# An attention layer's projections and value products with 512-column matmuls over both parts, the halves added afterwards, and its head transposes three steps behind

## The chip, the cores and the metric

The kernel runs on one core of a Trainium2 chip. The metric is the device time of one execution in microseconds, as the median of several runs. The core has five instruction streams: PE (TensorE, matmuls, with its weight loads shown apart as PEld), DVE (VectorE), ACT (ScalarE), POOL (GpSimd) and SP (which issues transfers). Each works through its own stream in order and waits for the others at semaphores.

## The reference

One inference step of a backbone of two layers over 9 tiles of 128 tokens: tile 0 is the context (128 tokens of a new request), tiles 1 to 8 are 1024 latent tokens. Layer 0 mixes tokens with retention and pooling, layer 1 with grouped-query attention; each is followed by a SwiGLU feed-forward part. The change lies in layer 1's attention:

```python
def attn_project(h, w_qkv, q_gain, k_gain):
    q, k, v = jnp.split(h @ w_qkv, [N_HEADS * HEAD_DIM, (N_HEADS + KV_HEADS) * HEAD_DIM], axis=-1)
    q = rmsnorm(q.reshape(B, T, N_HEADS, HEAD_DIM), q_gain)      # 8 heads of 128
    k = rmsnorm(k.reshape(B, T, KV_HEADS, HEAD_DIM), k_gain)     # 2 heads of 128
    v = v.reshape(B, T, KV_HEADS, HEAD_DIM)
    return q, k, v
...
qs, ksl = axial_rope(qs), axial_rope(ksl)                        # latent tokens only
k_all = jnp.concatenate([cache_k[:, j], ksl], axis=1)            # 256 cached + 1024 keys
v_all = jnp.concatenate([cache_v[:, j], vs], axis=1)
os_ = block_attention(qs, k_all, v_all) @ w_o[j]                 # softmax(q k^T * scale) v
```

The context tile attends to itself alone, and its normed keys and its values are outputs.

## The kernel before, in words

**Two parts.** The kernel works in float32, but its large matmuls use a faster format that keeps fewer bits. So every large operand is split into a high and a low part (`split`: ACT writes `hi`, a rounded copy; DVE writes `lo`, the source minus `hi`), and a product becomes three matmuls: high by high, high by low and low by high (`mm3`, whose matmul is line 182). A matmul takes a stationary operand of 128 x 128 and streams a moving operand of up to 512 columns past it. `mm3` accumulates all three products in the same columns of a PSUM bank. Layer 0 also uses another form, `mm_wide` (matmul on line 191): where the high and the low part of the moving operand lie at a fixed distance, one matmul with the high part as the stationary operand streams both, 256 + 256 columns, into the two halves of a bank; a second one, with the low part as the stationary operand, streams the high 256 columns into the first half. The halves are added when they are read (`add2`, lines 637 and 638: an ACT copy of one half to SBUF, then a DVE sum with the other half).

**Projections.** `blocks` lists six blocks of 256 output columns: `v`, q heads 0 and 1, `k`, and three more pairs of q heads. For each block and each of the 9 tiles, `qkv_step(bi, t)` multiplies the tile's hidden state (eight groups of 128 rows, in `h_hi`, `h_lo`) by the block's weights (`w_pair`) with `mm3`, 24 matmuls of 256 columns, into one of four banks in turn (in the last block banks 3 and 7). Blocks 0 and 1 are interleaved in groups of three tiles; the others follow one another. For `v` the result is then split into `VH`, `VL`. For `k` and `q`, ACT squares the result per head with an accumulator (line 1194), POOL makes the reciprocal root (`rstd_of`, lines 195 and 196), DVE scales the result into a buffer `qn` (line 1201), and the rotary part follows: a DVE product (1209), a POOL product (1210) and two DVE sums (1212, 1213). Then `qn` has to be transposed per head: `tail` does two PE transposes (line 1217) into bank 6 or 7 and a copy (line 1226) or split. The tail isn't issued at once but appended to `pend`, and a step issues the oldest tail behind its own matmuls when more than one is pending, so two steps later than its own. The buffers of `qn` rotate through three (`qnb`), those of the rotary parts through two (`rab`).

Between the projections stand side tasks: cached keys (`cached_k`) and values, and the context's own attention for each pair of heads (`ctx_pair`, at the places in `ctx_at`). In the last block, the first scores of the main loop are already issued (`q_split(0)`, `scores(0, ...)`).

**Attention.** The main loop runs over 32 `pairs` (8 tiles by 4 pairs of heads). For each: `q_split` on POOL; `scores`, per head, 9 or so matmuls over 1280 keys into two and a half banks, a DVE row maximum (1308), an ACT exponential (1310), a scaling on ACT (1315) or DVE (1313); `p_trans`, five calls of four transposes (1326) and a split, whose ACT copy is line 159 and whose DVE part is line 160; and `values`, five calls for 256 keys each, which accumulate over all five in bank 7, six matmuls of 256 columns in a call. After the last, an ACT copy (line 1344) takes bank 7 to `O`. The order within a pair is written out by hand, and runs into the pair before:

```python
for w in 'T0 v3 S0 T1 v4 T2 S1 T3 V0 V1 T4 V2'.split():
```

T is `p_trans`, S `scores` of the next pair, V `values` of this pair and v of the pair before.

**Order.** The order of the program is a priority. A scheduler at build time goes through it with modelled durations and gives each engine a fixed order, in which an instruction that is ready by the model can pass one that is not. It also sets the semaphores. Any two engines that use the same PSUM bank are kept apart.

Of the kernel before, what the change touches and what calls it, by code (L numbers as in the profile page):

```python
# [64 lines left out]
def hybrid_step_kernel(ctx: ExitStack, tc: tile.TileContext, a: dict, outs: list):  # L65
# [45 lines left out]
    def bank(i, n=1):  # L111
        return PS[:, i * 512:(i + n) * 512]
# [1037 lines left out]

    rope = XG[:, 0:2048].rearrange("p (t x) -> p t x", t=8)
    vctx = XG[:, 2048:2304]
    qnb = [XG[:, 2304 + 256 * i:2560 + 256 * i] for i in range(3)]
    rab = [XG[:, 3072 + 512 * i:3584 + 512 * i] for i in range(2)]
    kctx = T[:, 0:256]
    GQ = T[:, 512:768]
    jnk = [T[:, 256 + 128 * i:384 + 128 * i] for i in range(2)]
    VH = M2[:, 0:2048].rearrange("p (t e) -> p t e", t=8)
    VL = M2[:, 2048:4096].rearrange("p (t e) -> p t e", t=8)
    KR = M1.rearrange("p (v x s) -> p v x s", v=2, x=2)  # L1160
# [6 lines left out]
    pend = []  # L1167

    def qr_buf(bi, t, n):
        q, r = qnb[n % 3], rab[n % 2]  # L1170
        if bi == 5 and t > 3:
            q, r = RAW[:, 0, 256 * (n % 3):256 * (n % 3) + 256], RAW[:, 1, 512 * (n % 2):512 * (n % 2) + 512]
        return q, r[:, 0:256], r[:, 256:512]

    def qkv_step(bi, t):
        kind = blocks[bi][0]
        hi, lo = w_pair(2 * (bi % 2))
        g, j = divmod(t, 3)
        js = slice(j * 128, (j + 1) * 128)
        ps = bank(cnt["n"] % 4 if bi < 5 else 3 if t % 2 else 7)[:, 0:256]  # L1180
        cnt["n"] += 1
        mm3(ps, [(h_hi(g)[:, k, js], h_lo(g)[:, k, js], hi[:, k], lo[:, k]) for k in range(KD)])
        if len(pend) > 1:
            pend.pop(0)()
        if kind == "v":
            if t == 0:
                nc.scalar.copy(vctx, ps)
                nc.gpsimd.dma_start(out=new_cv[0, 0].rearrange("t v d -> t (v d)"), in_=vctx)
            else:
                split(VH[:, t - 1], VL[:, t - 1], ps)  # L1190
            return
        ss = sm(2)
        for e in range(2):
            nc.scalar.activation(jnk[e], ps[:, e * 128:(e + 1) * 128], ACTF.Square, accum_out=ss[:, e:e + 1])
        r = rstd_of(ss, 128, 2)
        cnt["q"] += 1
        n_qn = cnt["q"]
        qn, ra, rb = qr_buf(bi, t, n_qn)
        gain = GQ[:, 128:256] if kind == "k" else GQ[:, 0:128]
        for e in range(2):  # L1200
            nc.vector.scalar_tensor_tensor(qn[:, e * 128:(e + 1) * 128], ps[:, e * 128:(e + 1) * 128], r[:, e:e + 1],
                                           gain, op0=ALU.mult, op1=ALU.mult)
        if t == 0:
            if kind == "k":
                nc.gpsimd.dma_start(out=new_ck[0, 0].rearrange("t v d -> t (v d)"), in_=qn)
        else:
            v3 = lambda x: x.rearrange("p (h d) -> p h d", h=2)
            tb = rope[:, t - 1]
            nc.vector.tensor_mul(v3(ra), v3(qn), tb[:, 0:128].unsqueeze(1).to_broadcast([128, 2, 128]))
            nc.gpsimd.tensor_mul(v3(rb), v3(qn), tb[:, 128:256].unsqueeze(1).to_broadcast([128, 2, 128]))  # L1210
            v4 = lambda x: x.rearrange("p (q x i) -> p q x i", q=4, x=2)
            nc.vector.tensor_add(v4(qn)[:, :, 0], v4(ra)[:, :, 0], v4(rb)[:, :, 1])
            nc.vector.tensor_add(v4(qn)[:, :, 1], v4(ra)[:, :, 1], v4(rb)[:, :, 0])
        def tail(qn=qn, kind=kind, t=t, n=n_qn):
            tp = bank(6 + n % 2 if NT * bi + t < 4 * NT + 6 else 6)[:, 0:256]
            for e in range(2):
                nc.tensor.transpose(tp[:, e * 128:(e + 1) * 128], qn[:, e * 128:(e + 1) * 128], ident)
            tp3 = tp.rearrange("p (h s) -> p h s", h=2)
            if kind == "k":
                if t == 0:  # L1220
                    nc.scalar.copy(kctx, tp)
                else:
                    cs = slice(256 + (t - 1) * 128, 256 + t * 128)
                    split(KR[:, :, 0, cs], KR[:, :, 1, cs], tp3)
            else:
                nc.scalar.copy(O[:, 2 * kind:2 * kind + 2, t * 128:(t + 1) * 128], tp3)

        pend.append(tail)
# [103 lines left out]
    def values(n, u):  # L1332
        t, hp = pairs[n]
        v = hp // 2
        op = bank(7)[:, 0:256]
        b = pts.pop((n, u))
        ph, pl = b[:, 0:512], b[:, 512:1024]
        for jj in range(2):
            j = 2 * u + jj
            vs = slice(v * 128, (v + 1) * 128)  # L1340
            lh, ll = (CVH[:, j, vs], CVL[:, j, vs]) if j < 2 else (VH[:, j - 2, vs], VL[:, j - 2, vs])
            mm3(op, [(lh, ll, ph[:, jj * 256:jj * 256 + 256], pl[:, jj * 256:jj * 256 + 256])], j == 0, j == 9)
        if u == 4:
            nc.scalar.copy(O[:, 2 * hp:2 * hp + 2, t * 128:(t + 1) * 128], op.rearrange("p (h s) -> p h s", h=2))

    for g in range(NG):
        for bi in range(2):
# [5 lines left out]
    load_blk(2)  # L1353
    load_blk(3)
    side = {(3, 2): cached_k, (5, 1): cached_v}
    ctx_at = [(4, 0), (4, 3), (4, 6), (5, 2)]
    cf = []
    for bi in range(2, 6):
        for t in range(NT):
# [75 lines left out]
```

## Time and profile before

| | |
|---|---|
| median of 3 runs | 2875.98 us (2875.55 to 2877.53) |
| profiled execution | 2876.07 us |
| its span, first to last instruction | 2874.2 us |
| granted TensorE clock, mean | 0.996 |
| PE busy | 2818.4 us (98%), 17403 matmuls |
| DVE busy | 1804.4 us (63%) |
| ACT busy | 1080.3 us (38%) |
| POOL busy | 299.0 us (10%) |

A row of the timeline gives the start in us from the span's beginning, the length from the first start to the last end of a merged group, the engine, the line, the operation, the operands' names, the shape of the first one and the count. In square brackets stands idle time of the engine ahead of it, with what ended it. A row of the view by line or shape gives the count, the busy time, the mean duration of one, and the idle time ahead. A row of the windows gives, for a stretch of time, each engine's busy time with its count, then the granted clock, the DMA engines' share and the GB/s. Matmuls overlap, so their durations add up to more than the time they take together.

### The profile page before, as it was taken

The numbers are of one execution on the slowest core, as the hardware profiler recorded it, in microseconds if no ns is written. First come the engines' busy times: TensorE is split into PE (matmuls) and PEld (weight loads), VectorE is DVE, ScalarE is ACT, GpSimd is POOL, SyncE is SP. The second block draws the span as 40 slices with busy tenths as digits, with TensorE's granted clock in tenths as the row PEclk, the third lists the DMA queues.
The fourth block names the chain that finished last, engine by engine and source line by source line (L and its number), as shares of the span: only waits on it lengthen the run. The fifth ranks groups of instructions, "written<-read, shape, count | busy, mean of one in ns | idle before, by whom it ended". The sixth has DMA issues, their size and how long they took to land. (4 is left out here: it accounts for less than half of the span.)

```text
span 2874.2 us, 43669 instructions
## 1 busy us (share of the span) xinstructions
PE 2818.4 (98%) x17403; PEld 2515.0 (88%) x17403; DVE 1804.4 (63%) x3044; ACT 1080.3 (38%) x2033; POOL 299.0 (10%) x542
## 2 busy tenths in 40 slices
PE   7999999999999999999999999999999999999998
PEld 5778888788999999977779988888889999998886
DVE  6784456536867676665765567885496555554455
ACT  5333323326322323331263367775362222234111
POOL 2010111111000000000034521110100000000000
PEclk9999999999999999999999999999999999999999
DMA  7531111412334333443341000001233222225222
GB/s 259 163 117 50 36 34 34 142 59 74 110 119 129 101 128 97 137 162 115 124 151 44 23 16 1 23 30 66 85 101 97 73 77 78 73 82 171 78 93 103
DMA packets 194565, 262.53 MB, mean 91 GB/s; under 512 B 10220, under 2 KB 139688, under 8 KB 194232
## 3 DMA queue, kind: packets, MB, share of 16 engines
q1 hardware_dynamic: 182784, 217.88, 24.0%
q0 software_dynamic: 11088, 41.47, 3.8%
q8 instruction: 137, 2.24, 0.3%
q14 instruction: 68, 0.56, 0.1%
q10 hardware_dynamic: 488, 0.38, 0.0%
HBM read 213.52 MB, written 46.17 MB: 90 GB/s over the span
## 5 line engine op out<-in xcount | busy, mean ns | idle before, releaser
L182 PE MATMUL PS<-RR 128*128 128x512 f32 (+2 forms) x4542 | 906.0, 349 | 1.9 <-ACT RR L159 0.7
L182 PEld LDWEIGHTS PS<-RR 128*128 128x128 f32 x4542 | 744.1, 189 | 104.0 <-issue 6.9
L875 PE MATMUL PS<-RR 128*128 128x288 f32 x5324 | 730.5, 296 | 3.4 <-ACT XGT L890 1.6
L875 PEld LDWEIGHTS PS<-RR 128*128 128x128 f32 x5324 | 714.4, 188 | 12.7 <-ACT O L357 5.9
L159 ACT CAST RR<-O 128x512 fp32r<-128x512 f32 (+1 forms) x242 | 152.3, 629 | 533.9 <-PE PS L875 459.8
L182 PE MATMUL PS<-RR,MID2True 128*128 128x256 f32 (+1 forms) x1416 | 269.1, 338 | 0.1
L1089 DVE TENSOR_TENSOR O<-PS,O 128x512 f32<-128x512 f32 x216 | 149.0, 690 | 173.1 <-PE PS L182 170.8
L182 PEld LDWEIGHTS PS<-RR,MID2True 128*128 128x128 f32 x1416 | 218.2, 189 | 30.1 <-DVE RR L160 0.6
L191 PE MATMUL PS<-RR 128*128 128x256 f32 (+1 forms) x1152 | 219.7, 345 | 0.0
L160 DVE TENSOR_TENSOR RR<-O,RR 128x512 fp32r<-128x512 f32 (+1 forms) x242 | 167.8, 694 | 73.7 <-ACT RR L159 73.7
L191 PEld LDWEIGHTS PS<-RR 128*128 128x128 f32 x1152 | 178.1, 188 | 35.5 <-issue 7.9
L359 DVE SCALAR_TENSOR_TENSOR O<-O,PW 128x512 f32<-128x512 f32 x224 | 160.2, 747 | 16.3 <-ACT O L357 9.2
L182 PE MATMUL PS<-MID1True,RR 128*128 128x512 f32 (+1 forms) x630 | 166.6, 372 | 2.2 <-ACT XGT L1310 1.7
L159 ACT CAST RR<-RAW 128x512 fp32r<-128x512 f32 (+1 forms) x119 | 95.6, 810 | 182.6 <-PE PS L875 87.7
L875 PE MATMUL PS<-MID1True,RR 128*128 128x288 f32 x1100 | 159.9, 295 | 0.0
L875 PEld LDWEIGHTS PS<-MID1True,RR 128*128 128x128 f32 x1100 | 150.9, 189 | 0.0
L875 PE MATMUL PS<-MID2True,RR 128*128 128x288 f32 x968 | 147.0, 295 | 0.0
L160 DVE TENSOR_TENSOR RR<-RAW,RR 128x512 fp32r<-128x512 f32 (+1 forms) x119 | 110.6, 933 | 47.6 <-ACT RR L159 45.0
L195 POOL TENSOR_SCALAR SM<-SM 128x1 f32<-128x1 f32 (+1 forms) x153 | 55.4, 362 | 778.8 <-ACT PS L231 302.7
L875 PEld LDWEIGHTS PS<-MID2True,RR 128*128 128x128 f32 x968 | 135.5, 189 | 0.0
L906 POOL DMA_DIRECT2D gg<-XGT x44 | 23.6, 537 | 952.8 <-DVE XGT L905 952.8
L1308 DVE TENSOR_REDUCE SM<-PS 128x1 f32<-128x1280 f32 x64 | 95.5, 1491 | 40.4 <-PE PS L182 40.0
(300 smaller groups left out, 3338.0 us busy)
## 6 DMA issues: line engine op xcount, KB each, us to landing
O<-in_w_ada_dram SPq DMA_DIRECT2D x68, 512.0 KB
RAW<-in_w_ffn_in_dram SPq DMA_DIRECT2D x100, 256.0 KB
gg<-XGT POOLq DMA_DIRECT2D x44, 576.0 KB, 3.2
O<-in_w_ffn_in_dram SPq DMA_DIRECT2D x92, 256.0 KB
RAW<-in_w_ffn_out_dram SPq DMA_DIRECT2D x30, 512.0 KB
MID2False<-gg SPq DMA_DIRECT2D x26, 576.0 KB
RAW<-in_w_in_even_dram SPq DMA_DIRECT2D x28, 512.0 KB
x<-XGT POOLq DMA_DIRECT2D x27, 512.0 KB, 3.0
```

Of the source, the lines that this page charges most:

```text
L159: nc.scalar.copy(hi, src)
L160: nc.vector.tensor_sub(lo, src, hi)
L182: nc.tensor.matmul(out=out, lhsT=x, rhs=y, start=(first and c == 0), stop=(last and c == n - 1))
L191: nc.tensor.matmul(out=o, lhsT=x, rhs=y, start=(i == 0 and c == 0), stop=(i == n - 1 and c == 1))
L195: nc.gpsimd.tensor_scalar(r, ss, 1.0 / n, EPS, op0=ALU.mult, op1=ALU.add)
L359: nc.vector.scalar_tensor_tensor(self.acc[kind], b[:, k], sv, self.acc[kind], op0=ALU.mult, op1=ALU.add)
L875: nc.tensor.matmul(out=ps, lhsT=u[:, ks], rhs=v, start=first and n == 0, stop=n == 11, skip_group_check=not first)
L906: nc.gpsimd.dma_start(out=gg_scr[self.l][f], in_=XGT[:, 2880:4032])
L1089: nc.vector.tensor_add(dst, p3, dst)
L1308: nc.vector.reduce_max(nm, sp, axis=AX.X, negate=True)
```

## The change

Four things change, all in layer 1's attention.

- `qkv_step` uses `mm_wide` in place of `mm3`: per group of rows one matmul of 512 columns and one of 256 in place of three of 256, into a whole bank. Right behind it an ACT copy and a DVE sum bring the halves together in SBUF, in the buffer that later holds `qn` (for `v` in one of the rotary buffers, or `vctx`). The squares and the scaling read that buffer instead of the bank, and the squares write into the rotary buffer `ra` instead of `jnk`.
- A tail is issued when more than two are pending, three steps after its own. `qnb` gets a fourth buffer, in the place of `jnk`. The context's fourth pair moves from tile 2 to tile 3 of the last block.
- `values` uses the same wide form over the high and low parts of the transposed probabilities: per 128 keys one matmul of 512 and one of 256 columns. Bank 7 is then taken to `O` by an ACT copy of the second half and a DVE sum with the first.
- The loops, blocks, transfers and the order within a pair stay.

```diff
-    qnb = [XG[:, 2304 + 256 * i:2560 + 256 * i] for i in range(3)]
+    qnb = [XG[:, 2304 + 256 * i:2560 + 256 * i] for i in range(3)] + [T[:, 256:512]]
...
-    jnk = [T[:, 256 + 128 * i:384 + 128 * i] for i in range(2)]
...
-        q, r = qnb[n % 3], rab[n % 2]
+        q, r = qnb[n % 4], rab[n % 2]
         if bi == 5 and t > 3:
-            q, r = RAW[:, 0, 256 * (n % 3):256 * (n % 3) + 256], ...
+            q, r = RAW[:, 0, 256 * (n % 4):256 * (n % 4) + 256], ...
...
-        ps = bank(cnt["n"] % 4 if bi < 5 else 3 if t % 2 else 7)[:, 0:256]
+        ps = bank(cnt["n"] % 4 if bi < 5 else 3 if t % 2 else 7)
         cnt["n"] += 1
-        mm3(ps, [(h_hi(g)[:, k, js], h_lo(g)[:, k, js], hi[:, k], lo[:, k]) for k in range(KD)])
-        if len(pend) > 1:
+        ww = w_wide(2 * (bi % 2))
+        mm_wide(ps, [(h_hi(g)[:, k, js], h_lo(g)[:, k, js], ww[:, k], hi[:, k]) for k in range(KD)])
+        if kind == "v":
+            x = vctx if t == 0 else rab[t % 2][:, 0:256]
+        else:
+            cnt["q"] += 1
+            n_qn = cnt["q"]
+            x, ra, rb = qr_buf(bi, t, n_qn)
+        nc.scalar.copy(x, ps[:, 256:512])
+        nc.vector.tensor_add(x, ps[:, 0:256], x)
+        ps = x
+        if len(pend) > 2:
             pend.pop(0)()
         if kind == "v":
             if t == 0:
-                nc.scalar.copy(vctx, ps)
                 nc.gpsimd.dma_start(out=new_cv[0, 0].rearrange("t v d -> t (v d)"), in_=vctx)
...
-            nc.scalar.activation(jnk[e], ps[:, e * 128:(e + 1) * 128], ACTF.Square, accum_out=ss[:, e:e + 1])
+            nc.scalar.activation(ra[:, e * 128:(e + 1) * 128], ps[:, e * 128:(e + 1) * 128], ACTF.Square, accum_out=ss[:, e:e + 1])
...
-        qn, ra, rb = qr_buf(bi, t, n_qn)
+        qn = x
...
-        op = bank(7)[:, 0:256]
+        op = bank(7)
         b = pts.pop((n, u))
-        ph, pl = b[:, 0:512], b[:, 512:1024]
+        pw = b.rearrange("p (x j f) -> p j x f", x=2, j=2)
...
-            mm3(op, [(lh, ll, ph[:, jj * 256:jj * 256 + 256], pl[:, jj * 256:jj * 256 + 256])], j == 0, j == 9)
+            two_ = [(lh, pw[:, jj], op.rearrange("p (x f) -> p x f", x=2)), (ll, pw[:, jj, 0], op[:, 0:256])]
+            for i, (x, y, o) in enumerate(two_[::-1] if j == 9 else two_):
+                nc.tensor.matmul(out=o, lhsT=x, rhs=y, start=(j == 0 and i == 0), stop=(j == 9 and i == 1))
         if u == 4:
-            nc.scalar.copy(O[:, 2 * hp:2 * hp + 2, t * 128:(t + 1) * 128], op.rearrange("p (h s) -> p h s", h=2))
+            ov = O[:, 2 * hp:2 * hp + 2, t * 128:(t + 1) * 128]
+            nc.scalar.copy(ov, op[:, 256:512].rearrange("p (h s) -> p h s", h=2))
+            nc.vector.tensor_add(ov, op[:, 0:256].rearrange("p (h s) -> p h s", h=2), ov)
...
-    ctx_at = [(4, 0), (4, 3), (4, 6), (5, 2)]
+    ctx_at = [(4, 0), (4, 3), (4, 6), (5, 3)]
```

The wide projection's helper, which stays as it is:

```python
def mm_wide(out, items):
    n = len(items)
    for i, (lh, ll, rw, rh) in enumerate(items):
        two_ = [(lh, rw, out.rearrange("p (x f) -> p x f", x=2)), (ll, rh, out[:, 0:256])]
        for c, (x, y, o) in enumerate(two_ if i == 0 else two_[::-1]):
            nc.tensor.matmul(out=o, lhsT=x, rhs=y, start=(i == 0 and c == 0), stop=(i == n - 1 and c == 1))
```

More of the change, by code (lines that the diff above doesn't have):

```diff
@@ L1169, in qr_buf @@
     def qr_buf(bi, t, n):
-        q, r = qnb[n % 3], rab[n % 2]
+        q, r = qnb[n % 4], rab[n % 2]
         if bi == 5 and t > 3:
-            q, r = RAW[:, 0, 256 * (n % 3):256 * (n % 3) + 256], RAW[:, 1, 512 * (n % 2):512 * (n % 2) + 512]
+            q, r = RAW[:, 0, 256 * (n % 4):256 * (n % 4) + 256], RAW[:, 1, 512 * (n % 2):512 * (n % 2) + 512]
         return q, r[:, 0:256], r[:, 256:512]
@@ L1193, in qkv_step @@
         for e in range(2):
-            nc.scalar.activation(jnk[e], ps[:, e * 128:(e + 1) * 128], ACTF.Square, accum_out=ss[:, e:e + 1])
+            nc.scalar.activation(ra[:, e * 128:(e + 1) * 128], ps[:, e * 128:(e + 1) * 128], ACTF.Square, accum_out=ss[:, e:e + 1])
         r = rstd_of(ss, 128, 2)
-        cnt["q"] += 1
-        n_qn = cnt["q"]
-        qn, ra, rb = qr_buf(bi, t, n_qn)
+        qn = x
         gain = GQ[:, 128:256] if kind == "k" else GQ[:, 0:128]
```

## The prediction

> **What bounds the kernel now.** I read the page's busy times and chain first, then the matmuls by shape, then the stages' windows, then the timeline of the two stages that the change touches.
>
> ```profile
> PE 2818.4 (98%) x17403; PEld 2515.0 (88%) x17403; DVE 1804.4 (63%) x3044; ACT 1080.3 (38%) x2033; POOL 299.0 (10%) x542
> PE 38%; DVE 2%; ACT 1%; issue 1%; POOL 1%; POOLq 0%; DVEq 0%; ACTq 0%
> ...
> core 0: us, PE busy (x) PEld busy (x) DVE busy (x) ACT busy (x) POOL busy (x), PEclk, DMA share, GB/s
> ...
> 1514.00:1553.00 39.00, 39.00 (x331) 39.00 (x330) 21.72 (x56) 16.40 (x51) 11.15 (x19) 1.00 0.10 28
> 1663.00:1685.00 22.00, 18.75 (x125) 15.71 (x124) 13.01 (x30) 10.96 (x28) 8.31 (x14) 1.00 0.14 49
> 1685.00:1976.00 291.00, 291.00 (x2081) 261.07 (x2079) 230.09 (x315) 223.96 (x346) 32.62 (x57) 1.00 0.06 17
> ```
>
> TensorE is the bound, at full granted clock (1.00). The edited code runs from 1491 to about 1982 us (the last row shown below): projections to 1663, a seam of 22 us in which PE is idle for 3.25 us, then 291 us of attention where PE has no idle time and DVE (230.09) and ACT (223.96) are at 79% and 77%. So time can come only from cheaper PE work, or from the seam, and DVE and ACT are not far behind in the attention stage.
>
> The cost of a matmul is not its duration: matmuls overlap. It is the distance between starts.
>
> ```profile
> 1537.08 11.76 PE L182 MATMUL PS<-RR 128*128 128x256 f32 x96
> 1548.68 0.38 PE L1217 MATMUL PS<-CT,XGT 128*128 128x128 f32 x2
> 1548.81 0.36 PE L182 MATMUL PS<-RR 128*128 128x256 f32 x1
> ...
> 71.55 8.53 PE L191 MATMUL PS<-RR 128*128 128x512 f32 x48
> ...
> 1804.13 0.60 PE L1326 MATMUL PS<-CT,XGT 128*128 128x128 f32 x4
> 1804.49 0.96 PE L182 MATMUL PS<-RR,MID2True 128*128 128x256 f32 x6
> 1805.29 1.56 PE L182 MATMUL PS<-MID1True,RR 128*128 128x512 f32 x6
> 1806.68 0.72 PE L1326 MATMUL PS<-CT,XGT 128*128 128x128 f32 x5
> ```
>
> Narrow: four projection steps (96 matmuls of 256 columns) take 1548.68 - 1537.08 = 11.60 us to the next start. The first matmul behind a pair of head transposes also pays what the second transpose does not: two transposes take 0.13 us here (1548.68 to 1548.81), while a transpose more costs (0.60 - 0.38)/2 = 0.11 by the rows of four and of two, so 0.09 of the 11.60 belongs to them. 11.51/96 = 0.120 us each, 2.88 per step. Wide: the row of 48 at 71.55 is three steps of the form that the change brings, 24 matmuls of 512 and 24 of 256 columns (the timeline labels a merged group by its first shape). The six of 512 at 1805.29 let the next start at 1806.68: 1.39/6 = 0.232 each, and the last one hangs over by 1.56 - 1.39 = 0.17. So three wide steps last 8.53 - 0.17 = 8.36, 2.79 each, and the 256 ones among them cost (2.79 - 8 x 0.232)/8 = 0.117. Columns dominate and their number is the same; only a little overhead per instruction goes.
>
> **The change part by part.**
>
> *Projections.* 6 blocks x 9 tiles = 54 steps, each 24 narrow matmuls before, 8 wide and 8 narrow after: 2.88 - 2.79 = 0.09, times 54 is 4.9 us, all on PE, which is the bound. Ends: 0.06 a step (3.2) if the 256 ones keep their 0.120 beside the wide ones (8 x 0.352 = 2.82); 0.11 a step (5.9) by the uncorrected 2.90. I take 4.9.
>
> *Value products.* 32 head pairs x 5 calls. A call is 6 narrow ones: from the transposes at 1804.13 to the next group at 1805.29 are 1.16 us, less 4 x 0.11, so 0.72. After: 2 x (0.232 + 0.117) = 0.70. 0.02 x 160 = 3.2 us by these rounded rows; 0.71 in place of 0.72 would give 1.6. I take 2.0, ends 0.7 and 3.5.
>
> The Trainium skill, "TensorE: Matmul & The Clock Gate", section "Back-to-back issue gap", speaks against both: at full clock a matmul's spacing is its columns over 2.4 GHz plus some 2.5 ns, which is 0.109 for 256 and 0.216 for 512. By that a step goes from 2.62 to 2.60 and a call gains 5 ns, an estimate of 1.9 us in place of my 6.9. The trace disagrees with both figures (0.120, 0.232), so its rows stand.
>
> *The new copies and sums.* Each projection step gains an ACT copy and a DVE sum of 128x256; each pair gains a sum behind the copy it already has. The same two operations stand in the earlier mixer, and the lines they join are these:
>
> ```profile
> L637 ACT COPY MID1False<-PS x36: 352/372/376, 74.5 to 415.5; 128x256 f32<-128x256 f32 x36
> L638 DVE TENSOR_TENSOR MID1False<-PS,MID1False x36: 405/424/426, 75.2 to 416.0; 128x256 f32<-128x256 f32 x36
> ...
> L1194 ACT ACTIVATE XGT<-PS x90: 266/279/310, 1507.8 to 1676.0; 128x128 f32<-128x128 f32 x90
> L1194 ACT ACTIVATION_READ_ACCUMULATOR XGT<-PS x90: 194/203/231, 1508.0 to 1676.2; 128x1 f32 x90
> ...
> 1564.07 0.61 DVE L1201 SCALAR_TENSOR_TENSOR XGT<-PS,SM,XGT 128x128 f32<-128x128 f32 x2 [0.66 <-POOL SM L196]
> 1564.71 0.43 DVE L1209 TENSOR_TENSOR XGT<-XGT 128x256 f32<-128x256 f32 x1
> 1564.76 0.98 POOL L1210 TENSOR_TENSOR XGT<-XGT 128x256 f32<-128x256 f32 x1 [0.73 <-DVE XGT L1201]
> 1565.77 0.29 DVE L1212 TENSOR_TENSOR XGT<-XGT 128x128 f32<-128x128 f32 x1 [0.63 <-POOL XGT L1210]
> 1565.82 0.29 POOL L195 TENSOR_SCALAR SM<-SM 128x2 f32<-128x2 f32 x1
> 1566.18 0.42 DVE L160 TENSOR_TENSOR MID1True<-PS,MID1True 128x256 fp32r<-128x256 f32 x1
> 1566.20 0.70 POOL L196 TENSOR_TENSOR SM<-SM,PW 128x2 f32<-128x2 f32 x1
> 1566.93 0.61 DVE L1201 SCALAR_TENSOR_TENSOR XGT<-PS,SM,XGT 128x128 f32<-128x128 f32 x2 [0.33 <-POOL SM L196]
> ```
>
> In the key block, the heaviest, DVE repeats every 1566.93 - 1564.07 = 2.86 us, of which 0.63 + 0.33 are waits for POOL. PE's step with its two transposes is 2.88 + 0.22 = 3.10 now and becomes 3.01. The 0.42 fits into the 0.63 wait if it is put there; put behind the scaling it would make 3.28, and DVE would set the pace for some steps until the lag moves the sum into the wait. The lag is covered by the third step of distance: from a matmul's end to its transposes the chain is copy 0.37, sum 0.42, two squares with their accumulators 0.96, POOL 0.99, scaling 0.61, product 0.98, two sums 0.58: 4.9, with handovers under 6 us, and three steps are 9. With two steps (6 us) there would be no cover; that is what the moved tail, the fourth buffer in T and the context pair moved from tile 2 to 3 pay for. Zero on PE. The SP queue is untouched; the new-key and new-value stores on POOL's queue wait some 0.8 us longer, and nobody waits for them.
>
> The Trainium skill, "SBUF — State Buffer", "Who interferes with whom", says that a VectorE instruction with two SBUF inputs and a GpSimd one that reads SBUF block each other. The scaling (L1201) gets its second SBUF input by this change. No row here shows it by itself: POOL's product takes 0.98 beside DVE's product of two SBUF inputs, and never stands alone. But POOL starts only when the scaling has ended (1564.76), so I add nothing.
>
> *Banks.* The sum frees a projection's bank about 1 us after its matmuls, earlier than the scaling did. The opposite: the tail of tile 5 of block 4 uses bank 7 and now stands just ahead of the projection that takes bank 7 (block 5, tile 0). It must wait for a copy, or its place is taken by the next tile's: 0 to 0.7 us, I take 0.3.
>
> *The seam.*
>
> ```profile
> 1669.96 1.09 PE L182 MATMUL PS<-MID1True,RR 128*128 128x256 f32 x5 [0.90 <-ACT XGT L1310]
> 1673.71 0.98 PE L182 MATMUL PS<-MID1True,RR 128*128 128x512 f32 x3 [0.52 <-DVE RAW L1201]
> 1678.31 0.86 PE L182 MATMUL PS<-MID1True,RR 128*128 128x256 f32 x4 [0.76 <-ACT XGT L1310]
> 1679.89 0.41 PE L1217 MATMUL PS<-CT,RAW 128*128 128x128 f32 x2 [0.73 <-DVE RAW L1213]
> ```
>
> The 0.52 is a bank held by the scaling; it should go. Late next: the last tail (0.73) has a chain 0.8 us longer and three tails in place of two at the end. Ends: all 2.9 us gone, or 1.5 more. I take -0.5.
>
> *Attention.* Bank 7 is now held for copy and sum:
>
> ```profile
> 1805.54 0.38 ACT L1344 COPY O<-PS 128x256 f32<-128x256 f32 x1 [0.18 <-PE PS L182]
> 1805.74 1.28 DVE L160 TENSOR_TENSOR RR<-PS,RR 128x512 fp32r<-128x512 f32 x2
> 1807.31 0.16 DVE L1311 RECIPROCAL SM<-SM 128x1 f32<-128x1 f32 x1 [0.29 <-ACT XGT L1310]
> 1807.79 0.49 PE L1326 MATMUL PS<-CT,XGT 128*128 128x128 f32 x3
> 1807.99 1.49 DVE L1308 TENSOR_REDUCE SM<-PS 128x1 f32<-128x1280 f32 x1 [0.52 <-PE PS L182]
> 1808.04 0.72 PE L182 MATMUL PS<-RR 128*128 128x256 f32 x4
> ```
>
> The copy ends at 1805.92, DVE's two splits at 1807.02, so the sum runs to about 1807.44, and the next pair's first value product, at 1808.04, has 0.6 us left; the row maximum starts at 1807.99 as before. I add nothing; the ends are -1 and +13 (a rival below).
>
> Sum: -4.9 - 2.0 - 0.5 + 0.3 = -7.1. The profiled execution took 2876.07 (span 2874.2 and 1.87 around it), 0.09 above the median of 2875.98. 2876.07 - 7.1 = 2869.0.
>
> **The rivals.** Within 0.2%, which is 5.75 us, is about what this measurement cannot tell from no change.
>
> *No change.* PE's saving in attention turns into waits, since the transposes already wait for DVE: of the five at 1806.68 the last is followed only at 1807.33, (1807.33 - 1806.68) - 5 x 0.11 = 0.10 late. DVE gets 0.42 more per pair, so PE keeps its period, and projections lose half their gain to DVE's 2.86 us loop: -2.5 to -4, about 2873. The 79% of DVE speaks for it, the 0.6 us of slack against. The two kernels would also be that near by the skill's spacing.
>
> *Slower.* In attention the order of DVE is written ahead by the scheduler. If the sum is put before the second split, that split ends 0.42 later, at 1807.44. The fifth transpose at 1806.68 already belongs to the third group (a group has four, and three follow at 1807.79), starts at 1806.68 + 4 x 0.11 = 1807.12 and needs the bank that this split frees: 0.3 to 0.4 late with the handover, in 32 pairs up to +13, less 7.1, about 2882. It decides from 0.22 us per pair on (7.1/32). For it: the copy is done at 1805.92, before the second split starts (about 1806.4, half way through the 1.28). Against: the split is issued earlier in the program.
>
> *Much faster.* The durations taken at face:
>
> ```profile
> L182 PE MATMUL PS<-RR 128*128 128x256 f32 x1488 | 198.7, 287 | 0.0
> L191 PE MATMUL PS<-RR 128*128 128x512 f32 x576 | 209.3, 407 | 0.0
> L191 PE MATMUL PS<-RR 128*128 128x256 f32 x576 | 151.5, 283 | 0.0
> ```
>
> 24 x 0.287 = 6.9 against 8 x (0.407 + 0.283) = 5.5 per step, and 1.72 against 1.38 per value call, would save 74 + 54 us: 2748. The 96 matmuls in 11.76 us rule it out; a gain beyond 15 us would need a wide matmul well under 0.232, which no row shows. The same section of the skill also gives a sustained 131 ns for 512 columns, which would point this way; the trace's 232 disagrees.
>
> **How the numbers follow.** Forecast 0.50 (its own range 2865 to 2872), no change 0.32, slower 0.15, much faster 0.03. The range runs from 2863 (the gain ends together, 5.9 + 3.5 + 2.9 and a little) to 2878, which takes in all of "no change" and the start of "slower". The forecast counts as faster: 0.53, 0.32, 0.15.
>
> **What would show it.** A projection step with its tail every 3.01 us instead of 3.10; the copy at 0.37 and the sum at 0.42 on it; no wait of PE for the scaling in the seam; a value call of 0.70; and the 32 output copies, now 1691.1 to 1982.0, in some 2 us less. It is wrong if PE waits appear before head transposes or before a value product, if the transposes in attention move apart, or if the scheduler's new order costs PE in the seam more than 2 us.
>
> ```profile
> L1344 ACT COPY O<-PS x32: 372/375/376, 1691.1 to 1982.0; 128x256 f32<-128x256 f32 x32
> ```

## The result, and the profile after

The changed kernel takes 2916.16 us in the median (2914.04 to 2917.33) against 2876.03 beside it: a ratio of 1.0136, 95% interval 1.0124 to 1.0147. The forecast was 2869.0 with a range to 2878. It is slower by 40 us, with the sign wrong.

The page's busy times of the kernel after:

```profile
PE 2829.6 (97%) x16651; PEld 2487.1 (85%) x16651; DVE 1831.6 (63%) x3130; ACT 1098.2 (38%) x2086; POOL 291.9 (10%) x542
```

Nothing here says what happened: PE still has 97% and DVE gains 27 us in a span that is 41 longer. The windows of the edited stages do:

```profile
core 0: us, PE busy (x) PEld busy (x) DVE busy (x) ACT busy (x) POOL busy (x), PEclk, DMA share, GB/s
...
1514.00:1560.00 46.00, 43.13 (x253) 37.45 (x252) 25.82 (x68) 19.84 (x61) 11.25 (x18) 0.96 0.08 23
1560.00:1614.00 54.00, 39.66 (x213) 32.59 (x211) 32.36 (x89) 18.94 (x82) 23.89 (x39) 0.95 0.13 40
1614.00:1636.00 22.00, 22.00 (x130) 19.14 (x130) 9.75 (x32) 8.94 (x34) 9.29 (x16) 0.97 0.06 19
1636.00:1700.00 64.00, 53.07 (x282) 43.79 (x282) 34.44 (x103) 25.47 (x116) 28.40 (x48) 0.92 0.02 5
1700.00:1726.00 26.00, 17.72 (x89) 14.63 (x88) 13.96 (x34) 11.47 (x34) 8.62 (x15) 0.91 0.00 1
1726.00:2022.00 296.00, 295.86 (x1822) 254.63 (x1822) 243.21 (x352) 230.00 (x354) 33.14 (x58) 1.00 0.08 25
```

Projections and seam now reach to about 1726 instead of 1685. PE is busy for 43.13 + 39.66 + 22.00 + 53.07 + 17.72 = 175.6 of 212 us, so idle for 36.4. Before, in the same stage, it was idle for some 4 (148.08 of 149 by the row below, and the 3.25 of the seam). The granted clock falls to between 0.91 and 0.97. Attention has almost no idle time, and the first and last output copies there are 286.7 us apart, against 290.9:

```profile
L1353 ACT COPY O<-PS x32: 372/373/374, 1736.0 to 2022.7; 128x256 f32<-128x256 f32 x32
```

So attention became shorter, and the whole loss lies in the projections. Before:

```profile
1514.00:1663.00 149.00, 148.08 (x1235) 146.98 (x1234) 87.30 (x244) 58.79 (x248) 78.19 (x121) 1.00 0.09 27
```

The list of PE's waits in the kernel after names the place (engine, line, what it waited for, us in all, times, longest). Line 1223 is the head transposes, 1248 those of the cached keys, 182 the scores. What they wait for is line 160, DVE's part of a split, 1219, the second rotary sum, and 1316, the exponential:

```profile
PE PS L1223 <- DVE MID1True L160: 7.0, 5, 2.0
...
PE PS L1223 <- DVE XGT L1219: 5.8, 5, 1.4
PE PS L182 <- ACT XGT L1316: 5.3, 1, 5.3
...
PE PS L1248 <- DVE MID1True L160: 4.1, 1, 4.1
```

Why DVE is late is seen in the timeline of one step, here of a query block after the change. Line 1207 is the scaling, 1215 DVE's product, 1218 and 1219 the rotary sums, 1190 the new sum, 1202 the squares, and 195 and 196 the root. DVE's rows come first, then those of ACT and POOL inside the same step:

```profile
1617.31 0.62 DVE L1207 SCALAR_TENSOR_TENSOR XGT<-XGT,SM 128x128 f32<-128x128 f32 x2 [1.82 <-POOL SM L196]
1617.96 0.43 DVE L1215 TENSOR_TENSOR XGT<-XGT 128x256 f32<-128x256 f32 x1
1619.02 0.29 DVE L1218 TENSOR_TENSOR XGT<-XGT 128x128 f32<-128x128 f32 x1 [0.63 <-POOL XGT L1216]
1619.23 0.28 DVE L1219 TENSOR_TENSOR XGT<-XGT 128x128 f32<-128x128 f32 x1
1619.43 0.42 DVE L1190 TENSOR_TENSOR XGT<-PS,XGT 128x256 f32<-128x256 f32 x1
1621.67 0.62 DVE L1207 SCALAR_TENSOR_TENSOR XGT<-XGT,SM 128x128 f32<-128x128 f32 x2 [1.82 <-POOL SM L196]
...
1619.88 0.31 ACT L1202 ACTIVATE XGT<-XGT 128x128 f32<-128x128 f32 x1 [1.15 <-DVE XGT L1190]
...
1620.66 0.19 POOL L195 TENSOR_SCALAR SM<-SM 128x2 f32<-128x2 f32 x1 [1.68 <-ACT XGT L1202]
1620.94 0.69 POOL L196 TENSOR_TENSOR SM<-SM,PW 128x2 f32<-128x2 f32 x1
```

Follow the circle. DVE scales tile s (1617.31), does its product, waits for POOL's product and does the two rotary sums. Only then comes the new sum of tile s+1 (1619.43). The squares of s+1 wait for it (ACT, 1619.88), the root for the squares (POOL, 1620.66 to 1621.63), and DVE's next scaling for the root, 1.82 us idle. Around once: 1621.67 - 1617.31 = 4.36 us. Before, the squares read the bank directly behind the matmuls, so the next root was made beside the rotary part, and the circle was 2.86. PE needs about 3.03. None of the engines on the circle is full: in the window from 1614 to 1636 DVE is busy for 9.75 of 22 us, ACT for 8.94 and POOL for 9.29. The step is set by pieces that follow one another.

The kernel after has the short circle too, at the few places where the scheduler put the sum elsewhere. At the last tile of the key block the sum stands right behind the scaling, ahead of DVE's product, and the next scaling comes 2.83 us later, not 4.36:

```profile
1602.77 0.61 DVE L1207 SCALAR_TENSOR_TENSOR XGT<-XGT,SM 128x128 f32<-128x128 f32 x2 [0.87 <-POOL SM L196]
1603.30 0.42 DVE L1190 TENSOR_TENSOR XGT<-PS,XGT 128x256 f32<-128x256 f32 x1
...
1605.60 0.61 DVE L1207 SCALAR_TENSOR_TENSOR XGT<-XGT,SM 128x128 f32<-128x128 f32 x2 [0.39 <-POOL SM L196]
```

The three steps of distance hide the long circle for a while. From 1617.88 to 1633.06 PE does its head transposes every 3.04 us, without a pause, while DVE falls back by 1.3 us a step; then the lead is spent, and PE waits (1.34 us at 1638.04). In the key block, earlier, it is spent already, and the head transposes come every 4.35 us instead of 3.03:

```profile
1586.80 0.44 PE L1223 MATMUL PS<-CT,XGT 128*128 128x128 f32 x2 [1.09 <-DVE MID1True L160]
...
1591.15 0.44 PE L1223 MATMUL PS<-CT,XGT 128*128 128x128 f32 x2 [1.09 <-DVE MID1True L160]
...
1600.83 0.44 PE L1223 MATMUL PS<-CT,XGT 128*128 128x128 f32 x2 [2.05 <-DVE MID1True L160]
1601.02 4.60 PE L191 MATMUL PS<-RR 128*128 128x512 f32 x16
```

The last row is a second effect: the matmuls of a step, 3.07 us at 1586.99, take 4.60 here, at a lower clock.

Blocks 2 to 5 are 36 steps. From DVE's scaling of the tile ahead of them to the last scaling pass 156.5 us (1565.14 to 1721.60), on average 4.35 a step, though single steps beside tile 0 and the side tasks take between 2.77 and 8.70. Before the change these were 122.6 us (1554.85 to 1677.49), 3.41 a step. So the four blocks lose 33.8 us. The scaling ahead of them is 10.3 us late already; the first two blocks have steps of 4.35 too (1540.00 to 1544.35), but what else is in the 10.3 was not worked out. Together that is 44.1, the first output copy comes 44.9 later (1736.0 against 1691.1), and attention gives 4.2 of it back.

### The profile page after: what moved, and what is told of

It reads as the page before. It is cut to its first block, busy times and chain, and to the rows that moved or that the text cites. A ratio compares the mean times of both kernels' runs of the same rounds, so it can differ in the third digit from the quotient of the medians.

```text
span 2915.6 us, 42268 instructions
## 1 busy us (share of the span) xinstructions
PE 2829.6 (97%) x16651; PEld 2487.1 (85%) x16651; DVE 1831.6 (63%) x3130; ACT 1098.2 (38%) x2086; POOL 291.9 (10%) x542
## 3 DMA queue, kind: packets, MB, share of 16 engines
q1 hardware_dynamic: 182784, 217.88, 23.7%
## 5 line engine op out<-in xcount | busy, mean ns | idle before, releaser
L875 PEld LDWEIGHTS PS<-RR 128*128 128x128 f32 x5324 | 716.4, 189 | 12.2 <-ACT O L357 5.9
L182 PE MATMUL PS<-RR 128*128 128x512 f32 (+1 forms) x3054 | 707.5, 380 | 1.2 <-ACT O L1087 0.6
L182 PEld LDWEIGHTS PS<-RR 128*128 128x128 f32 x3054 | 560.4, 188 | 103.0 <-issue 6.9
L191 PE MATMUL PS<-RR 128*128 128x512 f32 x2016 | 391.0, 349 | 1.6 <-ACT O L1232 0.8
L191 PEld LDWEIGHTS PS<-RR 128*128 128x128 f32 x2016 | 316.6, 192 | 56.7 <-issue 7.9
L182 PE MATMUL PS<-RR,MID2True 128*128 128x512 f32 x648 | 157.9, 399 | 0.5 <-ACT RR L159 0.4
L875 PEld LDWEIGHTS PS<-MID1True,RR 128*128 128x128 f32 x1100 | 150.9, 189 | 0.0
L182 PEld LDWEIGHTS PS<-RR,MID2True 128*128 128x128 f32 x648 | 120.7, 188 | 31.2 <-ACT RR L159 1.2
L182 PEld LDWEIGHTS PS<-MID1True,RR 128*128 128x128 f32 x630 | 107.6, 191 | 25.3 <-ACT XGT L1316 6.2
```

The lines of the kernel that those rows point to most:

```text
L182: nc.tensor.matmul(out=out, lhsT=x, rhs=y, start=(first and c == 0), stop=(last and c == n - 1))
L191: nc.tensor.matmul(out=o, lhsT=x, rhs=y, start=(i == 0 and c == 0), stop=(i == n - 1 and c == 1))
L875: nc.tensor.matmul(out=ps, lhsT=u[:, ks], rhs=v, start=first and n == 0, stop=n == 11, skip_group_check=not first)
```

## The experiments

The theory was the circle through DVE. The rivals: the distance of the tails; the 512-column matmuls themselves; the additional work of copy and sum, wherever it stands; the lowered clock.

| kernel | median us | before beside it | ratio (95%) |
|---|---|---|---|
| value products only | 2873.26 | 2876.62 | 0.9985 (0.9976 to 0.9994) |
| projections only | 2918.89 | 2876.62 | 1.0147 (1.0133 to 1.0161) |
| no copy, no sum | 2869.09 | 2876.62 | 0.9972 (0.9961 to 0.9983) |
| narrow matmuls, same halves | 2918.25 | 2876.62 | 1.0144 (1.0128 to 1.0159) |
| tails two steps behind | 2915.08 | 2876.47 | 1.0133 (1.0117 to 1.0148) |
| norm later | 2875.08 | 2876.47 | 0.9995 (0.9987 to 1.0004) |
| squares from the bank | 2919.15 | 2876.47 | 1.0149 (1.0135 to 1.0162) |
| squares of the copied half | 2869.77 | 2876.97 | 0.9974 (0.9962 to 0.9986) |
| norm later, to the end | 2869.10 | 2876.97 | 0.9973 (0.9961 to 0.9984) |
| the same, last tails in attention | 2869.21 | 2876.97 | 0.9972 (0.9961 to 0.9983) |
| filled with matmuls | 2924.88 | 2876.97 | 1.0164 (1.0150 to 1.0178) |
| only the rotary part later | 2874.05 | 2876.89 | 0.9989 (0.9980 to 0.9998) |

**The two halves of the change apart.** First the kernel before with the new `values` (the last hunk but one of the change's diff, and nothing else of it):

> The value products alone are wide; projections and tails as in the kernel before. Theory (the loss lies in the projections, where DVE's sum joins a loop): 1 to 2 us faster than before, about 2874.5, the 32 output copies some 1 us closer together, no new wait of PE. Rival (the sum on bank 7 holds up the next pair, and the rest of the loss is there): slower than before by several us, with waits of PE for DVE in attention.

Then the kernel after with the old `values` (all of the diff but that hunk):

> The projections with wide matmuls, sums and three-step tails; the value products as before. Theory: the whole loss, 40 to 42 us over before, about 2917, and the DVE scalings 4.35 us apart. Rival (loss in the attention stage): less than 20 us over before.

The value products alone gain 3.4 us, more than the 1 to 2 that were expected; the projections alone lose 42, as expected. Output copies with the value products alone:

```profile
L1347 ACT COPY O<-PS x32: 372/372/373, 1690.6 to 1978.3; 128x256 f32<-128x256 f32 x32
```

They are 287.7 us apart, against 290.9 before: 3.2 of the 3.4 lie in attention.

**Without copy and sum.** The 512-column matmuls and the three steps stay; the squares and the scaling read the first half of the bank, and the second half's product is left out of the result.

```diff
-        nc.scalar.copy(x, ps[:, 256:512])
-        nc.vector.tensor_add(x, ps[:, 0:256], x)
-        ps = x
+        ps = ps[:, 0:256]
```

> The changed kernel, but the ACT copy and the DVE sum of the projections are left out: only the first half of each bank is read, so the product of the high part of the hidden state with the low part of the weights is missing from q, k and v. All matmuls, banks, buffers and the three-step tails stay. Theory (the sum in DVE's order makes the loop): the scalings return to PE's pace, PE waits between 1514 us and the attention fall to a few us, no half-clock windows there; about 2868, 7 us below before. Rival (wide matmuls, whole banks or the tails' distance cost PE the time): stays above 2905.

2869.09: the loss is gone, and what is left is the gain of the wide matmuls. So copy and sum together are the cause; in which way is left to the runs below. In its timeline the head transposes and DVE's scalings:

```profile
1549.64 0.38 PE L1222 MATMUL PS<-CT,XGT 128*128 128x128 f32 x2
...
1558.73 0.38 PE L1222 MATMUL PS<-CT,XGT 128*128 128x128 f32 x2
...
1628.84 0.61 DVE L1206 SCALAR_TENSOR_TENSOR XGT<-PS,SM,XGT 128x128 f32<-128x128 f32 x2 [0.66 <-POOL SM L196]
...
1631.69 0.61 DVE L1206 SCALAR_TENSOR_TENSOR XGT<-PS,SM,XGT 128x128 f32<-128x128 f32 x2 [0.66 <-POOL SM L196]
```

Three steps from 1549.64 to 1558.73 are 3.03 each, and DVE's circle is 2.85 again.

**The matmuls narrow, the halves kept apart.** Three matmuls of 256 columns per row group, one of them into the second half, then the same copy and sum:

```diff
-        mm_wide(ps, [...])
+        for k in range(KD):
+            three = [(lh, hi[:, k], ps[:, 0:256]), (lh, lo[:, k], ps[:, 256:512]), (ll, hi[:, k], ps[:, 0:256])]
+            ...
```

> The changed kernel with narrow matmuls in the projections: three of 256 columns, the one with the weights' low part into the second half of the bank, so copy, sum, buffers and tails stay exactly as changed, and no 512-column matmul is left there. Theory (the sum makes the loop, whatever PE does): still 35 us or more over before, about 2914, scalings still 4.35 us apart, since DVE sets the pace and PE's 0.09 us a step does not count. Rival (the 512-column form is at fault): back to about 2876.

2918.25, about as slow as the change: the wide matmuls have no part in the loss.

**The tails at a distance of two steps again:**

```diff
-        if len(pend) > 2:
+        if len(pend) > 1:
```

> The changed kernel with tails at two steps again; four buffers and the rest as changed. Theory (a loop of 4.35 us per step against 3.0 of PE, whatever the distance): the lag that the distance forgives is spent once per stretch of steps, so one step less costs one more wait of some 3 us per stretch, 3 to 15 us over the changed kernel, and the scalings stay 4.35 us apart. Rival (the chain of one step is longer than the distance, and each step waits for it by itself): one step less costs up to 3 us in each of the 45 steps, 60 us or more over the changed kernel.

2915.08, 1 us less than the change, where the theory had expected 3 to 15 more: in this it missed. PE now waits behind line 1219 for 23.7 us in 21 pieces, against 5.8 in 5, but DVE's circle is as long as before, with 155.8 us over the same 36 steps (1563.56 to 1719.33). Distance is a store that is filled once; a circle that is too long in every step empties any distance. It decides when PE waits, and here not when the stage ends.

**The norm one step later.** The squares, root, scaling and rotary part of a tile are issued behind the next tile's sum, except in the last five tiles:

```diff
+        if late_norm:
+            with tc.issue_after(done.ins):     # done: the sum of this tile
+                late_norm.pop(0)()
...
+        late_norm.append(lambda: norm(...))
+        if bi == 5 and t > 3:
+            late_norm.pop(0)()
```

> The changed kernel in full, but squares, root, scaling and rotary part of a step are issued behind the sum of the next step (DVE's part is held behind that sum), except in the last five tiles of the last block. DVE's order per step has the same instructions in the same cycle; only the sum now runs one step ahead of the scaling that follows it. Theory (the sum closed a loop through squares and root): the scalings return to PE's pace, 3.0 us, PE waits mostly go, about 2870, below before and near the kernel without the sum. Rival (DVE has simply 0.42 us more per step than it can carry beside the waits for POOL, or two engines get in each other's way): stays above 2890.

In this kernel the late squares overwrite the result of value tiles 3 and 6, whose buffer they share. It takes 2875.08, 41 us less than the change. That is 5 above the expected 2870. The remainder is in the last five tiles, which kept the old order, as the run with the late norm to the end of the block shows further down. In the seam, from 1663 to 1690, PE is busy for 20.70 of 27 us, so idle for 6.3, at a clock of 0.87.

**The squares from the bank**, as before the change, of the first half only, so that the sum should be out of the circle:

```diff
+        half = ps[:, 0:256]
...
-            nc.scalar.activation(ra[...], ps[:, e * 128:(e + 1) * 128], ACTF.Square, ...)
+            nc.scalar.activation(ra[...], half[:, e * 128:(e + 1) * 128], ACTF.Square, ...)
```

> The changed kernel, but the squares read the first half of the bank instead of the sum, so the root lacks the product with the weights' low part; copy, sum and the rest stay in place and in DVE's order. This cuts the loop at one link, sum to squares. Theory: the root runs beside the rotary part again, DVE's cycle falls from 4.35 to about 3.3 us (2.86 before the change plus 0.42 of the sum), still over PE's 3.0 but little; 2868 to 2885. Rival (the sum's own time, or copy and sum holding the bank): 2905 or more.

A miss: 2919.15. The timeline says why, ACT first, then DVE:

```profile
1625.69 0.28 ACT L1203 ACTIVATE XGT<-PS 128x128 f32<-128x128 f32 x1 [2.45 <-DVE XGT L1190]
...
1625.24 0.42 DVE L1190 TENSOR_TENSOR XGT<-PS,XGT 128x256 f32<-128x256 f32 x1
1627.41 0.61 DVE L1208 SCALAR_TENSOR_TENSOR XGT<-XGT,SM 128x128 f32<-128x128 f32 x2 [1.75 <-POOL SM L196]
...
1631.80 0.35 DVE L1208 SCALAR_TENSOR_TENSOR XGT<-XGT,SM 128x128 f32<-128x128 f32 x1 [1.75 <-POOL SM L196]
```

The squares need no result of the sum any more and still wait for it for 2.45 us: both read the same bank, and the build keeps two engines on one bank apart, in the order of the program, in which the squares come behind the sum. The circle is 4.39, unbroken. The Trainium skill, "PSUM — Partial Sum Buffer", "PSUM bank collisions raise a hardware error", tells of a compiler's scheduler that adds such a dependency between instructions of two engines on the same bank and the same 32 partitions, reads included; the wait of 2.45 us here agrees.

So it is not enough to free the squares from the sum's result while they stand behind it on its bank. The next kernel moves them off the bank and ahead of the sum at once; which of the two would do alone was not tested. **The squares of the copied half**: they read what ACT has just written to SBUF, and stand ahead of the sum.

```diff
         nc.scalar.copy(x, ps[:, 256:512])
+        (squares of x, and the root)
         nc.vector.tensor_add(x, ps[:, 0:256], x)
```

> The squares read the half that ScalarE has just copied to SBUF, and are issued ahead of the sum, so that neither the sum nor its bank stands between a tile's matmuls and its root. The root therefore sees one half alone, and the normalisation of this layer has other values; the work on each engine is the same. Theory (the loop sum, squares, root, scaling closes over DVE): the root of the next tile runs beside the rotary products of this one, DVE's work per step is 0.61 + 0.42 + 0.63 + 0.57 + 0.42 = 2.65 us, PE sets the pace with 3.03, scalings stand 3.0 to 3.3 us apart, and the time is 2868 to 2880. Rival (the early squares of the last run failed because the added copy and sum themselves are too much for DVE or ACT): scalings stay above 4 us apart and the time above 2905.

```profile
1626.79 0.62 DVE L1208 SCALAR_TENSOR_TENSOR XGT<-XGT,SM 128x128 f32<-128x128 f32 x2 [0.63 <-POOL SM L196]
1627.44 0.43 DVE L1216 TENSOR_TENSOR XGT<-XGT 128x256 f32<-128x256 f32 x1
1628.50 0.29 DVE L1219 TENSOR_TENSOR XGT<-XGT 128x128 f32<-128x128 f32 x1 [0.64 <-POOL XGT L1217]
1628.71 0.28 DVE L1220 TENSOR_TENSOR XGT<-XGT 128x128 f32<-128x128 f32 x1
1628.91 0.42 DVE L1195 TENSOR_TENSOR XGT<-PS,XGT 128x256 f32<-128x256 f32 x1
1629.88 0.61 DVE L1208 SCALAR_TENSOR_TENSOR XGT<-XGT,SM 128x128 f32<-128x128 f32 x2 [0.55 <-POOL SM L196]
```

DVE does the same five groups in the same order with the same durations, at 3.09 us a step instead of 4.36, and the time is 2869.77. This is the clearest of the runs: the work on each engine stayed, the link from sum to squares went, and 46 us with it. The root sees only one half here, so this shows the cause and is no version to use.

**The late norm to the end of the last block**, with the other of the two buffers for the value tiles:

```diff
-            x = vctx if t == 0 else rab[t % 2][:, 0:256]
+            x = vctx if t == 0 else rab[(t + 1) % 2][:, 0:256]
...
         late_norm.append(lambda: norm(...))
-        if bi == 5 and t > 3:
-            late_norm.pop(0)()
...
+    late_norm.pop(0)()
     for f in pend:
         f()
```

> The normalisation and the rotary products of a tile are issued one step later, behind the sum of the next tile, now for every tile to the end of the last block; the value tiles use the other of their two buffers. Theory: no loop over DVE is left, the step keeps PE's 3.03, and the stretch before the attention is at least as short as without the sums: 2868 to 2872, faster than before by 0.15 to 0.3%. Rival (the late order only moves the waits into the seam, where the last tile's chain is longer by a step): 2873 to 2877, no change against before.

2869.10, faster than before by 0.27%. DVE's order is now sum, scaling, product, rotary sums, with no root to wait for:

```profile
1626.80 0.42 DVE L1191 TENSOR_TENSOR XGT<-PS,XGT 128x256 f32<-128x256 f32 x1 [0.56 <-ACT XGT L1190]
1627.14 0.61 DVE L1215 SCALAR_TENSOR_TENSOR XGT<-XGT,SM 128x128 f32<-128x128 f32 x2
...
1663.00:1685.00 22.00, 19.34 (x110) 14.99 (x109) 16.11 (x33) 13.85 (x30) 7.06 (x12) 1.00 0.13 48
```

In the seam PE is idle for 2.7 us, less than before. With the last two tails moved into attention besides:

```diff
-    for f in pend:
-        f()
+    pend.pop(0)()
...
                 p_trans(n, u)
+                if u == 4 and pend:
+                    pend.pop(0)()
```

> The kernel with the late normalisation, and with the transposes of the last two tiles put into the first two steps of the attention, behind its fifth group of transposes, as nothing needs them before the last tiles' scores. Theory: the seam loses its last wait of PE (some 4 us in the kernel with the late normalisation), so 1 to 4 us less than that kernel, about 2866 to 2870. Rival (the seam waits for the split of the first scores anyway, and the transposes of attention begin no earlier): equal to that kernel within 1 us.

2869.21: equal, where the theory had 1 to 4 us less. Those tails cost nothing where they were, as the rival had it.

**Is it the clock?** Five more matmuls of 512 columns at the head of each step of blocks 2 to 5, into the bank that the real ones then overwrite:

```diff
+        if bi > 1:
+            for i in range(5):
+                nc.tensor.matmul(out=ps..., lhsT=h_hi(g)[:, i, js], rhs=ww[:, i], start=True, stop=True)
         mm_wide(ps, [...])
```

> The kernel after, with five more 512-column matmuls at the head of each projection step of the last four blocks (36 steps), whose result is overwritten: 5 x 0.232 = 1.16 us more of PE per step, 41.8 us in all. Theory (DVE's loop of 4.35 us sets the pace, and both the waits of PE and its halved clock lie inside that): PE's step becomes 3.03 + 1.16 = 4.19, still under 4.35, and the time stays within 6 us of 2916 (2912 to 2922), with the waits gone from the list and the clock near 1.00. Rival 1 (the halved clock costs time by itself, about 13 us): a PE without pauses keeps its clock, and the time falls to 2900 to 2908. Rival 2 (PE's own work sets the time): 2916 + 41.8 = 2958.

```profile
1636.00:1700.00 64.00, 64.00 (x361) 54.93 (x359) 32.66 (x95) 27.51 (x112) 27.77 (x46) 1.00 0.02 5
...
1621.22 0.38 PE L1226 MATMUL PS<-CT,XGT 128*128 128x128 f32 x2
1625.42 0.38 PE L1226 MATMUL PS<-CT,XGT 128*128 128x128 f32 x2
...
1624.28 0.61 DVE L1210 SCALAR_TENSOR_TENSOR XGT<-XGT,SM 128x128 f32<-128x128 f32 x2 [1.81 <-POOL SM L196]
1628.62 0.61 DVE L1210 SCALAR_TENSOR_TENSOR XGT<-XGT,SM 128x128 f32<-128x128 f32 x2 [1.82 <-POOL SM L196]
```

From 1636 to 1700 PE has no pause and the full clock, and the kernel is not faster: 2924.88, 8.7 over the change and 3 beyond the bound that the theory gave. Both rivals are out, the one with 2900 to 2908 and the one with 2958. Of 41.8 us of additional work 33 vanished in the waits. PE steps are 4.20 apart and DVE's scalings still 4.34, at the full clock as at the lowered one. So neither PE's work nor its clock sets the length of the circle. With 4.20 PE is nearly as slow as the circle itself, and the side tasks come on top; whether the 8.7 lie there was not followed up.

**Only the rotary part moved.** Squares, root and scaling stay in their own step; the product, POOL's product and the rotary sums go behind the next tile's sum.

```diff
+        if late_rot:
+            with tc.issue_after(done.ins):     # done: the sum of this tile
+                late_rot.pop(0)()
...
+        late_rot.append(lambda: rot(...))      # the lines from the product to `pend.append(tail)`
```

> The kernel after with one thing moved: a tile's rotary part (DVE's product, POOL's product, two DVE sums) is issued behind the sum of the next tile instead of ahead of it; squares, root and scaling stay in their own step, directly behind the tile's sum. The value tiles use the other of their two buffers. Nothing is added or left out. Theory (the loss is the place of the sum in DVE's order: behind the rotary sums it makes a loop of 4.35, behind the scaling alone the loop is sum 0.42, squares and root 1.82, scaling 0.61, about 2.9): scalings follow PE at about 3.03 us, no wait of PE before head transposes in the key and query blocks, 2867 to 2873. Rival (DVE is short of time whatever the order, or the next sum comes late once PE sets the pace and the rotary part is pushed back behind it): scalings 3.3 us apart or more, 2880 to 2910.

2874.05, 1 us above the theory's range and far from the rival's. This order makes the circle 2.90 (1621.09 to 1623.99), in the rows of DVE and of POOL's product:

```profile
1621.09 0.61 DVE L1211 SCALAR_TENSOR_TENSOR XGT<-XGT,SM 128x128 f32<-128x128 f32 x2 [1.82 <-POOL SM L196]
1621.62 0.42 DVE L1191 TENSOR_TENSOR XGT<-PS,XGT 128x256 f32<-128x256 f32 x1
1621.79 0.74 POOL L1223 TENSOR_TENSOR XGT<-XGT 128x256 f32<-128x256 f32 x1 [0.73 <-DVE XGT L1211]
1621.95 0.85 DVE L1222 TENSOR_TENSOR XGT<-XGT 128x256 f32<-128x256 f32 x1
...
1623.99 0.61 DVE L1211 SCALAR_TENSOR_TENSOR XGT<-XGT,SM 128x128 f32<-128x128 f32 x2 [0.59 <-POOL SM L196]
```

The 42 us come back by moving 0.42 us of DVE from behind the rotary part to ahead of it, with nothing added or left out. It lacks 5 us to the version with the whole norm later. The first output copy comes 2.3 us later than there (1690.5 against 1688.2), with one wait of PE of 2.6 us before the cached keys' transposes, and the 32 copies lie 1.7 us further apart (288.8 against 287.1); why they do was not worked out.

## Why the prediction was wrong

**Right: the matmuls.** Projections were to give 4.9 (ends 3.2 to 5.9). In the kernel without the sums a step with its tail takes 3.03 instead of 3.10, where 3.01 was forecast: 0.07 x 54 = 3.8. Values were to give 2.0 (ends 0.7 to 3.5), and gave 3.4 alone. Without the copies and sums the kernel takes 2869.09, 7.5 less than before; the sum was -7.1. The much faster rival is out. So is the estimate of 1.9 us for both parts by the Trainium skill, "TensorE: Matmul & The Clock Gate", "Back-to-back issue gap": the runs give 3.8 and 3.4, nearly four times that.

**Right: attention.** PE is busy for 295.86 of 296 us there, so the slower rival, a late second split, did not occur; the output copies came closer by 4.2 us where 2 was forecast.

**Wrong: "the new copies and sums", zero on PE.** Three parts of that step failed. First, it priced the sum as 0.42 us of work to be fitted into DVE's idle time, and looked at two places for it: in the wait for POOL, or behind the scaling. The scheduler put it in a third for most of the steps, behind the rotary sums. Second, it never counted the sum as a link. The change moves the squares from the bank to `x`, so what had hung on PE alone now hangs on an instruction in DVE's queue that stands behind the rotary part of the tile before. The price of a wrong place is not 0.42 but the whole way from sum to root, 2.24 us (1619.43 to 1621.67) that no longer runs beside anything.

The durations were right: sum, squares and POOL add up to 2.37 in the prediction's chain. What they would run beside was wrong. The prediction had quoted the row that warned of it: before the change, too, DVE waited for the root (0.66) ahead of a scaling, so a root that starts later could only make that wait longer. Third, "until the lag moves the sum into the wait" supposed an order that adapts, while it is fixed at build time; and a lag pays a debt once, so "covered by the third step of distance" could not hold for 36 steps at 1.3 us each. It held for some six steps in the block shown above, and the run with two steps is as slow as the one with three. Whether the third step is of use once the circle is short was not run. What the runs show in place of the zero: with the same work and the link cut the kernel takes 2869.77, with only the rotary part behind the next sum 2874.05, so the way through the sum costs 42 to 46 us.

The number for the second place was off too, to the other side: behind the scaling the circle was to be 3.28, and it measures 2.83 in the change itself (1602.77 to 1605.60) and 2.90 in the last run. The 3.28 kept the wait of 0.63 for POOL's product, and in both places DVE has no such wait, since it is at the sum and at its own product in that time.

**Wrong by omission: the rivals.** "No change" did name DVE's circle in the projections, but at half of their gain, some 2.5 us, and "slower" lay in attention; both were priced as a contest for DVE's time. "PE waits before head transposes" stood under what would make it wrong, and that is what came (7.0 and 5.8 us), but with no price.

*Banks* and *the seam* are untested in the change itself, whose seam is drowned in the circle. In the version with the late norm PE idles for 2.7 us in the seam instead of 3.25, as far as that speaks for the -0.5.

## What to carry to other kernels

Where an engine with a fixed order gets a new instruction, ask first who waits for it and what stands ahead of it, and go around the circle once: a few tenths of a microsecond of work can close a loop over three engines, and none of them will look busy. If the loop is longer than the step, more distance between producer and consumer does not help; changing the order or cutting the link does. A link can also be a bank that two engines share, so take away every path before judging that a dependence was harmless.

## What the runs showed of the hardware

The granted clock fell without a long pause of PE. Windows of the kernel after around the slow step at 1601:

```profile
1597.00:1600.50 3.50, 1.77 (x11) 1.27 (x9) 3.47 (x8) 1.30 (x4) 0.98 (x1) 1.00 0.01 2
1600.80:1605.40 4.60, 4.58 (x18) 3.95 (x19) 3.54 (x8) 2.13 (x11) 2.92 (x5) 0.63 0.56 169
```

After 3.5 us in which PE was busy for half the time, with one wait of 2.05, the clock was 0.63 on average for the next 4.6 us, though PE was busy all through. The same follows at 1645, behind waits of 1.34, 1.27 and 2.18: a clock of 0.62 from 1645.2 to 1649.7. The Trainium skill, "TensorE: Matmul & The Clock Gate", "A second HAM failure mode: psum-queue depth-cycling", tells of a bf16 kernel whose frequent small pauses between groups of matmuls make the clock swing; the trace agrees as far as the pauses are small here too. What the lowered clock cost by itself is not shown. It did not set the circle: in the filled kernel the clock was 1.00 from 1636 to 1700, and DVE's scalings stood 4.34 us apart all the same.

The product of 128x256 on DVE took 0.43 when it began just ahead of POOL's product, which then took 0.98 (the prediction's rows at 1564.71 and 1564.76), and 0.85 in the rows of the last experiment, where POOL's had begun first and took 0.74 (1621.79). That the two share something is inferred from these durations; no run took POOL's product away. The Trainium skill, "SBUF — State Buffer", "Who interferes with whom", says that a VectorE instruction with two SBUF inputs contends with a GpSimd one that reads SBUF, and that the order of issue decides which one blocks; these durations agree. It did not lengthen the circle there: behind the longer product DVE still waited 0.59 us for the root (1623.99).
